# A two-layer hybrid attention kernel: gates moved between the forgetting attention's projections, row-alternating level products, decay rows copied by GpSimd, four equal statistics tiles

## The chip, the cores and the metric

The kernel runs on 1 core of one Trainium2 chip. The metric is the device time of one execution in microseconds (us). Before the change three runs took 1266.27, 1270.57 and 1270.88 us (median 1270.57). The profiled execution took 1268.24 us; its span, from the first to the last instruction, is 1266.4 us.

## The reference, cut to what matters

Everything is fp32. 16 meta tokens and 256 tokens (272 rows, 1024 wide) go through two layers. A layer is a feed-forward block, a token mixer and a second feed-forward block, each between two root-mean-square norms.

```
h = concatenate([meta, x])
for l in range(2):
    h = h + 0.5 * rmsnorm(swiglu(rmsnorm(h), w_ffn1_gu, w_ffn1_down))
    h = h + rmsnorm(token_mixer(rmsnorm(h), ...))
    h = h + 0.5 * rmsnorm(swiglu(rmsnorm(h), w_ffn2_gu, w_ffn2_down))
```

The mixer multiplies the normed rows by one wide matrix `w_in` and splits the product into queries, keys and values of two attentions and into three sets of gates:

```
log_f = log_sigmoid(ff + b_f)                      # 8 heads, forgetting attention ("fox")
s = q k^T / 8 + cum[q] - cum[k]                    # cum = cumsum(log_f)
o_fox = softmax(masked s) v
log_a = log_sigmoid(ga @ w_alpha_up + b_alpha)/16  # 4 heads, gated linear attention ("gla")
o_gla = chunked linear attention with a decay exp(cb[t] - cb[s]) per key channel
o_gla = rmsnorm(o_gla) * silu(gr)
y = sigmoid(g_merge_a) * (o_fox @ w_fox_o) + sigmoid(g_merge_b) * (o_gla @ w_gla_o)
return y @ w_out
```

## The kernel before

All activations lie transposed: 128 of the 1024 features on the partitions, the 272 rows (256 in the last layer's later part) along the free axis. A weight matrix comes by DMA in blocks of 128 x 1024 fp32 (SP's queue, `w`). Each half block of 512 columns is split into a rounded part (`wh`, an ACT cast, line 106) and the rest (`wl`, a DVE subtraction, line 112), and the operand likewise (`xh`, `xl`). A product of 128 features by 128 features is then three matmuls (`mm3`, lines 122 to 124: wh·xh, wh·xl, wl·xh), and a block makes 24 of them into one PSUM bank. Twelve half-block buffers let ACT and DVE run ahead of TensorE.

`inv_rms` makes a norm's factor. The squares of the features, already added up over the eight feature tiles, are summed over partitions by matmuls with a column of ones (line 171), so that the 272 sums land on partitions: two tiles of 128 and one of 16. DVE scales them (`ms`, line 179, once for the full tiles and once for the tile of 16), GpSimd raises them to -1/2 (`rp`, line 180), and matmuls against the identity (line 183) spread them over all partitions again. An fp32 matmul is two passes in the profile, a transpose one. `inv_rms` is called in `prep` (before each block of a layer, amid TensorE's projections) and in `Post.done` (after each block; there nothing else is left to do, and `idle` puts 5 and then 8 matmuls of no use around the broadcast). Of the eleven calls nine have 272 rows, two 256; the four of `Post.done` with 272 rows have two summands each.

The mixer's first four weight blocks give the decay inputs, the gla keys and half of its queries. After them comes a list `proj` of 37 blocks: the other half of the gla queries; for each of four head pairs the fox keys, queries and values; four blocks of gla values; the output gate `gr` (4); and the merge gates `ag` and `bg` (8 each, in turn). Each block's bank is emptied by one or two DVE instructions (lines 427, 436, 438, 450, 490). Two banks `mm` take turns, so a block waits until the block two before it has been emptied.

The attention's own steps are put between these blocks by `at(i, step)`: the step is written out just ahead of block i. `scores(b)` (line 645, the matmuls of two heads, then the softmax on DVE and ACT), `turn_fox`, `turn_scores` and `weigh` (the transposes and products with the values) stand three blocks apart for the four head pairs. `level(i)` makes the gla operand E of one of seven block widths L = 64 ... 1 on DVE and ACT; `products(i)` then multiplies its parts (line 562) and copies them into `att` by a mask. A head's operand has 64 rows: heads 0 and 2 lie on partitions 0 to 63, heads 1 and 3 on 64 to 127, r = 0 or 1 in the code. In layer 0 the levels of width 8 and less and `diagonal` (line 588) also have the 16 meta rows, whose stationary operand is 16 columns wide (lines 565 and 590). A scheduler with its own model of time then orders the instructions of every engine; each engine runs them in that order.

In `decays` the logarithms of the forget gates are made for 8 heads on partitions 32 to 39 and summed along the rows (the scan at line 416, `cf`). They enter the scores as extra rows of the contraction: `qa` has cum in rows 96 to 103 and marks in 64 to 71, `ka` has -cum (line 420) in 64 to 71 and marks in 96 to 103. Two DMAs issued by ACT (lines 421 and 422) spread these rows over 8 heads, so that scores contract over 104 rows, of which 48 are zeros or marks set by GpSimd (lines 344 to 347).

All sigmoids of the gates are put behind the last exponential by `follows`, so that ACT seldom changes its table.

## Time and profile before

| what | value |
|---|---|
| three runs | 1266.27, 1270.57, 1270.88 us |
| profiled execution, its span | 1268.24 us, 1266.4 us |
| TensorE (PE) busy | 1247.4 us, 99% |
| VectorE (DVE) busy | 893.4 us, 71% |
| ScalarE (ACT) busy | 697.5 us, 55% |
| GpSimd (POOL) busy | 34.9 us, 3% |
| TensorE's granted clock | 0.9 of full or more in every fortieth of the span |
| chain that ended last | PE 82%, "issue" 14%, DMA 1%, ACT 1% |

Matmuls are pipelined: one takes about 0.29 us from its start to its end, and the next starts about 0.125 us after it. A busy time of PE counts overlapped ends, so what an instruction costs is read from the distance between starts in the timeline, not from its duration.

### The profile page before, as it was taken

How to read it: one execution, taken by the hardware profiler on the slowest of the kernel's cores; microseconds unless marked ns; L12 is line 12 of the kernel's file. 1: busy time of each engine (PE TensorE's matmuls, PEld its weight loads, DVE VectorE, ACT ScalarE, POOL GpSimd, SP SyncE). 2: the span in 40 equal slices, each digit the busy share in tenths (PEclk: the TensorE clock that was granted, in tenths of full speed). 3: DMA queues.
4: the chain of work that ended last, by engine and by line, in shares of the span. 5: the costliest groups of instructions: out<-in, count | busy, mean ns of one | idle time of the engine just before them, and what ended most of it. 6: DMA issues, size and time to landing. Idle time of an engine off the chain costs nothing.

```text
span 1266.4 us, 25250 instructions
## 1 busy us (share of the span) xinstructions
PE 1247.4 (99%) x9826; PEld 1210.2 (96%) x9826; DVE 893.4 (71%) x1831; ACT 697.5 (55%) x1451; POOL 34.9 (3%) x43
## 2 busy tenths in 40 slices
PE   7999999999999999999999999999999999999997
PEld 7999999988999999999999999999898999999986
DVE  6777655887567787776568777558986687877662
ACT  7555544764555565554446555446755554755551
POOL 2000000000000100000000000001000000000000
PEclk9999999999999999999999999999999999999999
DMA  9655555443245636556536555564434564665650
GB/s 307 203 171 170 166 175 158 153 119 100 88 138 176 178 126 184 172 170 169 177 114 212 172 178 161 168 192 134 138 96 122 161 185 155 200 187 182 181 166 34
DMA packets 58198, 203.87 MB, mean 161 GB/s; under 512 B 6688, under 2 KB 8000, under 8 KB 58048
## 3 DMA queue, kind: packets, MB, share of 16 engines
q1 hardware_dynamic: 57376, 201.19, 51.7%
q8 instruction: 77, 1.26, 0.4%
q10 hardware_dynamic: 576, 0.80, 0.3%
q14 instruction: 41, 0.34, 0.1%
q0 software_dynamic: 128, 0.28, 0.1%
HBM read 200.92 MB, written 1.05 MB: 159 GB/s over the span
## 4 chain that ended last, share of the span: by engine, by line
PE 82%; issue 14%; DMA 1%; ACT 1%; POOL 0%; SPq 0%; ACTq 0%; DVE 0%; DVEq 0%; POOLq 0%
PE mm L122 13%; PE mm L124 12%; PE mm L123 12%; PE pp L122 7%; PE pp L124 7%; PE pp L123 7%; PE s L122 5%; PE s L123 5%; PE s L124 5%; PE pp L562 1%; PE s L161 1%; PE s L645 1%; DMA w<-in_w_gu 1%; PE po L183 1%; DMA ka<-sm 1%
## 5 line engine op out<-in xcount | busy, mean ns | idle before, releaser
L106 ACT CAST wh<-w 128x512 fp32r<-128x512 f32 (+1 forms) x768 | 464.6, 613 | 414.9 <-PE mm L123 183.8
L112 DVE TENSOR_TENSOR wl<-w,wh 128x512 fp32r<-128x512 f32 (+1 forms) x768 | 516.2, 681 | 246.4 <-ACT wh L106 231.0
L122 PE MATMUL mm<-xh,wh 128*128 128x272 f32 (+1 forms) x1072 | 309.4, 291 | 9.6 <-ACT wh L106 8.7
L124 PE MATMUL mm<-xh,wl 128*128 128x272 f32 (+1 forms) x1072 | 308.8, 289 | 0.0
L123 PE MATMUL mm<-xl,wh 128*128 128x272 f32 (+1 forms) x1072 | 307.8, 288 | 0.0
L122 PEld LDWEIGHTS mm<-xh,wh 128*128 128x128 f32 x1072 | 201.7, 189 | 11.7 <-ACT wh L106 8.9
L123 PEld LDWEIGHTS mm<-xl,wh 128*128 128x128 f32 x1072 | 202.9, 189 | 1.2 <-issue 0.9
L124 PEld LDWEIGHTS mm<-xh,wl 128*128 128x128 f32 x1072 | 202.2, 189 | 1.6 <-issue 1.1
L124 PE MATMUL s<-xh,wl 128*128 128x272 f32 (+1 forms) x496 | 142.2, 287 | 0.0
L123 PE MATMUL s<-xl,wh 128*128 128x272 f32 (+1 forms) x496 | 142.0, 287 | 0.0
L122 PE MATMUL s<-xh,wh 128*128 128x272 f32 (+1 forms) x496 | 141.0, 288 | 0.0
L124 PE MATMUL pp<-xh,wl 128*128 128x272 f32 (+1 forms) x480 | 137.2, 289 | 0.0
L123 PE MATMUL pp<-xl,wh 128*128 128x272 f32 (+1 forms) x480 | 137.0, 288 | 0.0
L122 PE MATMUL pp<-xh,wh 128*128 128x272 f32 (+1 forms) x480 | 134.0, 289 | 0.0
L123 PEld LDWEIGHTS s<-xl,wh 128*128 128x128 f32 x496 | 93.4, 188 | 0.1
L124 PEld LDWEIGHTS s<-xh,wl 128*128 128x128 f32 x496 | 93.4, 188 | 0.0
L122 PEld LDWEIGHTS s<-xh,wh 128*128 128x128 f32 x496 | 92.8, 188 | 0.1
L123 PEld LDWEIGHTS pp<-xl,wh 128*128 128x128 f32 x480 | 90.9, 189 | 0.0
L124 PEld LDWEIGHTS pp<-xh,wl 128*128 128x128 f32 x480 | 90.8, 190 | 0.0
L122 PEld LDWEIGHTS pp<-xh,wh 128*128 128x128 f32 x480 | 89.3, 190 | 0.0
L122 PE MATMUL pp<-hh,wh 128*128 128x272 f32 x264 | 76.1, 288 | 0.0
L122 PE MATMUL mm<-hh,wh 128*128 128x272 f32 x264 | 76.1, 288 | 0.0
(291 smaller groups left out, 2123.9 us busy)
## 6 DMA issues: line engine op xcount, KB each, us to landing
w<-in_w_gu SPq DMA_DIRECT2D x175, 512.0 KB, 3.6
w<-in_w_in SPq DMA_DIRECT2D x82, 512.0 KB, 3.6
w<-in_w_dn SPq DMA_DIRECT2D x48, 512.0 KB, 3.5
w<-in_w_end SPq DMA_DIRECT2D x22, 512.0 KB, 4.0
w<-in_w_dn SPq DMA_DIRECT2D x24, 384.0 KB, 3.5
w<-in_w_fg SPq DMA_DIRECT2D x16, 512.0 KB, 3.6
w<-in_w_o SPq DMA_DIRECT2D x16, 512.0 KB, 3.6
h<-in_xT SPq DMA_DIRECT2D x8, 136.0 KB, 4.7
```

Of the source, the lines that this page charges most:

```text
L106: i = nc.scalar.copy(wh[:, :n], w[:, a:b])
L112: nc.vector.tensor_tensor(wl[:, :n], w[:, a:b], wh[:, :n].bitcast(F32), ALU.subtract)
L122: nc.tensor.matmul(o, a, x[0], start=start, stop=False)
L123: nc.tensor.matmul(o, a, x[1], start=False, stop=False)
L124: nc.tensor.matmul(o, b, x[0], start=False, stop=stop)
L161: m = nc.tensor.matmul(o[:, :P], ident, ident, start=True, stop=True)
L183: last = nc.tensor.matmul(bc[:, o : o + m], rp[:m, j : j + 1].broadcast_to([m, P]), ident[:m, :m], start=True, stop=True)
L562: nc.tensor.matmul(pp[r][:, q * 64 : q * 64 + 64].rearrange("p (b l) -> p b l", l=L), x[:, o : o + P], second(x[:, o : o + P], L), start=T ...
L645: nc.tensor.matmul(s[:, c : c + e], qa[:104, hd, q0:e], ka[:104, hd, 0:e], start=True, stop=True)
```

## The change

`inv_rms` cuts 272 rows into four tiles of 68 (256 into two of 128 as before), needs one DVE instruction for all of them, and spreads the result by transposes instead of matmuls. `operands` and `decays` drop one of the two pairs of extra rows: `qa` has -1 marks in rows 64 to 71, `ka` has cum itself there, written by one GpSimd copy; scores contract over 72 rows. The memsets of rows 64 to 95, one marks DMA, the DVE negation and ACT's two DMAs go. In `products` and `diagonal` the loops go over tile, then head pair, then r, so that neighbouring matmuls lie on different halves of the partitions, and the meta rows' products use a stationary operand of 128 columns and come last. `proj` now puts one gate block after each pair of fox queries and keys and one after each block of values, and all `bg` blocks at the end; the fox steps stand five blocks apart, and the levels and the rest are given later places.

```diff
-        tt = [(o, min(P, n - o)) for o in range(0, n, P)]
-        J = len(tt)
+        m = P if n % P == 0 else n // 4
+        tt = range(0, n, m)
         st = bank("po")
         for i, part in enumerate(parts):
-            for j, (o, m) in enumerate(tt):
+            for j, o in enumerate(tt):
                 last = nc.tensor.matmul(st[:m, j : j + 1], part[:, o : o + m], one, start=i == 0 and j == 0,
...
-        for m, a, b in ((P, 0, n // P), (n % P, n // P, J)):
-            if m and b > a:
-                nc.vector.tensor_scalar(ms[:m, a:b], st[:m, a:b], q / D, q * EPS, ALU.mult, ALU.add)
-        nc.gpsimd.tensor_tensor(rp[:, :J], ms[:, :J], nhalf[:, :J], ALU.pow)
+        nc.vector.tensor_scalar(ms[:m, :J], st[:m, :J], q / D, q * EPS, ALU.mult, ALU.add)
+        nc.gpsimd.tensor_tensor(rp[:m, :J], ms[:m, :J], nhalf[:m, :J], ALU.pow)
         bc = bank("po")
-        for j, (o, m) in enumerate(tt):
-            last = nc.tensor.matmul(bc[:, o : o + m], rp[:m, j : j + 1].broadcast_to([m, P]), ident[:m, :m], start=True, stop=True)
+        for j, o in enumerate(tt):
+            last = nc.tensor.transpose(bc[:, o : o + m], rp[:m, j : j + 1].broadcast_to([m, P]), ident[:m, :m])
...
-        nc.gpsimd.memset(qa[64:96], 0.0)
-        nc.gpsimd.memset(ka[64:96], 0.0)
         nc.gpsimd.dma_start(qa[64:72], marks)
-        nc.gpsimd.dma_start(ka[96:104], marks)
...
-                cf = a[32:40, 2, :]
-                nc.vector.tensor_tensor_scan(cf, one[32:40].broadcast_to([8, NT]), b[32:40, 2, :], 0.0, ALU.mult, ALU.add)
+                    if f0 == 2:
+                        cf = a[rows, 2, :]
+                        nc.vector.tensor_tensor_scan(cf, one[rows].broadcast_to([8, NT]), b[rows, 2, :], 0.0, ALU.mult, ALU.add)
+                        nc.gpsimd.tensor_copy(ka[64:72], cf.unsqueeze(1).broadcast_to([8, FH, NT]))
...
-                nf = sm[32:40]
-                nc.vector.tensor_scalar(nf, cf, -1.0, None, ALU.mult)
-                nc.scalar.dma_start(qa[96:104], cf.unsqueeze(1).broadcast_to([8, FH, NT]))
-                nc.scalar.dma_start(ka[64:72], nf.unsqueeze(1).broadcast_to([8, FH, NT]))
...
+            def both_halves(ks):
+                return [(k, hh, r) for k in range(ks) for hh in range(2) for r in range(2)]
...
-                for hd in range(GH):
-                    r, hh = hd % 2, hd // 2
-                    x = head_rows(E, hd)
-                    for k in range(2):
-                        o = TILES[k + 1][0]
...
-                    if meta:
-                        nc.tensor.matmul(pp[r][:META, 256 + hh * 8 : 264 + hh * 8].rearrange("p (b l) -> p b l", l=L),
-                                         x[:, :META], second(x[:, :META], L), start=True, stop=True)
+                for k, hh, r in both_halves(2):
+                    x = E[64 * r : 64 * r + 64, hh]
+                    o = TILES[k + 1][0]
...
+                for _, hh, r in both_halves(meta):
+                    x = E[64 * r : 64 * r + 64, hh]
+                    nc.tensor.matmul(pp[r][:, 256 + hh * 8 : 264 + hh * 8].rearrange("p (b l) -> p b l", l=L),
+                                     x[:, :P], second(x[:, :META], L), start=True, stop=True)
...
-                        nc.tensor.matmul(s[:, c : c + e], qa[:104, hd, q0:e], ka[:104, hd, 0:e], start=True, stop=True)
+                        nc.tensor.matmul(s[:, c : c + e], qa[:72, hd, q0:e], ka[:72, hd, 0:e], start=True, stop=True)
...
+            gates = [(gate, gr, B_GR + i, i) for i in range(4)] + [(gate, ag, B_MA + i, i) for i in range(KC)]
+            gates.reverse()
             proj = [(gq1,)]
             for i in range(4):
-                proj += [(heads, ka, B_FK + i, i, None), (heads, qa, B_FQ + i, i, FD**-0.5), (values, B_FV + i, i)]
-            proj += [(values, B_GV + i, i) for i in range(4)]
-            proj += [(gate, gr, B_GR + i, i) for i in range(4)]
-            for i in range(KC):
-                proj += [(gate, ag, B_MA + i, i), (gate_b, i)]
+                proj += [(heads, ka, B_FK + i, i, None), (heads, qa, B_FQ + i, i, FD**-0.5), gates.pop(), (values, B_FV + i, i), gates.pop()]
+            for i in range(4):
+                proj += [(values, B_GV + i, i), gates.pop()]
+            proj += [(gate_b, i) for i in range(KC)]
...
-                at(5 + 3 * b, turn_fox, b)
-                at(5 + 3 * b, scores, b)
-                at(6 + 3 * b, turn_scores, b)
-                at(7 + 3 * b, weigh, b)
-            for i in range(len(LEVELS)):
-                at(6 + 2 * i, level, i)
-                at(7 + 2 * i, products, i)
-            at(20, diagonal)
+                at(5 + 5 * b, scores, b)
+                at(7 + 5 * b, turn_fox, b)
+                at(7 + 5 * b, turn_scores, b)
+                at(9 + 5 * b, weigh, b)
+            for i, j in enumerate((5, 7, 10, 12, 15, 17, 20)):
+                at(j, level, i)
+                at(j + 1, products, i)
+            at(23, between_decays)
+            at(23, diagonal)
...
-                at(23 + 2 * i, gla_values, k)
-                at(25 + 2 * i, gla_gate, k)
+                at(30 + 2 * i, gla_values, k)
+                at(32 + 2 * i, gla_gate, k)
```

On TensorE, the level of width 8 in layer 0. Before, with `pp_3776` and `pp_3777` the banks of r = 0 and r = 1, `E` the level's operand and `L667` the transposes of the fox scores:

```order
L562 MATMUL pp_3776<-E_3725 128x64 x2
L565 MATMUL pp_3776<-E_3725 16x8
L562 MATMUL pp_3777<-E_3725 128x64 x2
L565 MATMUL pp_3777<-E_3725 16x8
L562 MATMUL pp_3776<-E_3725 128x64
L667 MATMUL s_3711<-con_70,p_3637 128x128
L562 MATMUL pp_3776<-E_3725 128x64
L667 MATMUL s_3711<-con_70,p_3637 128x128 x2
L667 MATMUL s_3718<-con_70,p_3637 128x128
L565 MATMUL pp_3776<-E_3725 16x8
```

The same level now, from its sixth matmul to the projection that follows it (`pp_3720` and `pp_3721` are r = 0 and 1, L562 the meta rows):

```order
L558 MATMUL pp_3721<-E_3677 128x64
L558 MATMUL pp_3720<-E_3677 128x64
L558 MATMUL pp_3721<-E_3677 128x64
L562 MATMUL pp_3720<-E_3677 128x8
L562 MATMUL pp_3721<-E_3677 128x8
L562 MATMUL pp_3720<-E_3677 128x8
L562 MATMUL pp_3721<-E_3677 128x8
L120 MATMUL mm_3738<-xh_2755,wh_3645 128x272
```

The banks take turns, the meta rows' products are 128 wide and at the end, and the fox transposes stand elsewhere.

On DVE, from the forget gates' logarithms to the operands of the first two levels, layer 0, before (`G` is the gla decays' running sum, `ka_155<-mm_3205` empties the bank of the second block of fox keys' predecessor in turn):

```order
L414 TENSOR_TENSOR lsb_3071<-lsb_3071,lsa_3070 8x272
L112 TENSOR_TENSOR wl_3424<-w_3417,wh_3423 128x512
L416 SCALAR_TENSOR_TENSOR lsa_3070<-ones_71,lsb_3071 8x272
L414 TENSOR_TENSOR lsb_3071<-lsb_3071,lsa_3070 128x544
L420 TENSOR_SCALAR sm_2990<-lsa_3070 8x272
L112 TENSOR_TENSOR wl_3496<-w_3493,wh_3495 128x512
L436 TENSOR_TENSOR ka_155<-mm_3205,rs_2832 64x272 x2
L418 SCALAR_TENSOR_TENSOR G_2993<-ones_71,lsb_3071 128x272 x2
L112 TENSOR_TENSOR wl_3500<-w_3493,wh_3499 128x512
L525 TENSOR_TENSOR E_3327<-G_2993 128x2x2x64
L526 TENSOR_TENSOR E_3327<-G_2993 128x2x2x64
```

The same stretch now, from the forget gates' scan (L412) on (`vt` empties a block of fox values, `gr_3009<-mm_3274` the second output gate's block):

```order
L412 SCALAR_TENSOR_TENSOR lsa_3072<-ones_71,lsb_3073 8x272
L409 TENSOR_TENSOR lsb_3073<-lsb_3073,lsa_3072 128x544
L110 TENSOR_TENSOR wl_3483<-w_3480,wh_3482 128x512
L443 TENSOR_TENSOR vt_3232<-mm_3207,rs_2834 128x272
L415 SCALAR_TENSOR_TENSOR G_2995<-ones_71,lsb_3073 128x272 x2
L110 TENSOR_TENSOR wl_3487<-w_3480,wh_3486 128x512
L110 TENSOR_TENSOR wl_3528<-w_3525,wh_3527 128x512
L518 TENSOR_TENSOR E_3268<-G_2995 128x2x2x64
L519 TENSOR_TENSOR E_3268<-G_2995 128x2x2x64
L518 TENSOR_TENSOR E_3386<-G_2995 128x2x4x32
L519 TENSOR_TENSOR E_3386<-G_2995 128x2x4x32
L483 TENSOR_TENSOR gr_3009<-mm_3274,rs_2834 128x272
```

The negation is gone, and a gate's bank is emptied only after both levels' subtractions.

On TensorE, the sums after the mixer of layer 0 before (`sq` the squares, `s<-con` the idle matmuls):

```order
L171 MATMUL po_5636<-ones_71,sq_5595 128x1 x2
L171 MATMUL po_5636<-ones_71,sq_5595 16x1
L171 MATMUL po_5636<-ones_71,sq_5634 128x1 x2
L171 MATMUL po_5636<-ones_71,sq_5634 16x1
L161 MATMUL s_5643<-con_70 128x128 x5
L183 MATMUL po_5653<-con_70,rp_5649 128x128 x2
L183 MATMUL po_5653<-con_70,rp_5649 128x16
L161 MATMUL s_5657<-con_70 128x128 x8
```

And now:

```order
L169 MATMUL po_5636<-ones_71,sq_5595 68x1 x4
L169 MATMUL po_5636<-ones_71,sq_5634 68x1 x4
L159 MATMUL s_5645<-con_70 128x128 x5
L180 MATMUL po_5655<-con_70,rp_5652 128x68 x4
L159 MATMUL s_5660<-con_70 128x128 x8
```

Four tiles of one size stand where two of 128 and one of 16 stood; the rows L180 are transposes.

## Rows read from the trace of the kernel before

**Rows 1.** Page, part 1: busy us, share of the span, instructions of each engine.
```profile
PE 1247.4 (99%) x9826; PEld 1210.2 (96%) x9826; DVE 893.4 (71%) x1831; ACT 697.5 (55%) x1451; POOL 34.9 (3%) x43
```

**Rows 2.** Waits of PE: who waited for whom, us in total, times, longest.
```profile
PE s L645 <- DMA ka<-sm: 2.1, 2, 1.1
PE mm L122 <- DVE ka L436: 0.9, 2, 0.6
```

**Rows 3.** Timeline of PE, layer 0, level of width 4 (start us, us, instruction).
```profile
302.06 0.66 PE L562 MATMUL pp<-E 64*128 64x64 f32 x4
302.65 0.21 PE L565 MATMUL pp<-E 64*16 64x8 f32 x2
...
304.94 0.39 PE L122 MATMUL mm<-xh,wh 128*128 128x272 f32 x1
```

**Rows 4.** Timeline of PE, layer 1, level of width 1, without meta rows.
```profile
959.12 1.16 PE L562 MATMUL pp<-E 64*128 64x64 f32 x16
960.21 0.39 PE L122 MATMUL mm<-xh,wh 128*128 128x256 f32 x1
```

**Rows 5.** Timeline of PE, the diagonal products, layer 0 and then layer 1.
```profile
331.40 0.71 PE L588 MATMUL pp<-gq,gk 64*128 64x128 f32 x4
332.04 0.21 PE L590 MATMUL s<-gq,gk 64*16 64x16 f32 x2
...
334.52 0.39 PE L122 MATMUL mm<-xh,wh 128*128 128x272 f32 x1
...
963.24 1.26 PE L588 MATMUL pp<-gq,gk 64*128 64x128 f32 x16
```

**Rows 6.** Timeline of PE, the broadcast of the first norm's factor.
```profile
24.72 0.93 PE L183 MATMUL po<-con,rp 128*128 128x128 f32 x6
25.58 0.39 PE L122 MATMUL pp<-xh,wh 128*128 128x272 f32 x1
```

**Rows 7.** Timeline of PE, four transposes of 128 rows (line 762).
```profile
369.79 0.60 PE L762 MATMUL s<-con,on 128*128 128x128 f32 x4
370.15 0.37 PE L122 MATMUL mm<-xh,wh 128*128 128x272 f32 x1
```

**Rows 8.** Timeline of PE, the first norm's sums over partitions.
```profile
20.42 0.63 PE L171 MATMUL po<-ones,sq 128*128 128x1 f32 x6
20.98 0.39 PE L123 MATMUL mm<-xl,wh 128*128 128x272 f32 x1
```

**Rows 9.** Timeline of PE, layer 0, from behind the decay products to the first scores.
```profile
244.00 0.40 PE L123 MATMUL mm<-xl,wh 128*128 128x272 f32 x1
...
252.10 0.29 PE L123 MATMUL mm<-xl,wh 128*128 128x272 f32 x1
...
253.35 0.29 PE L124 MATMUL mm<-xh,wl 128*128 128x272 f32 x1
254.77 1.64 PE L645 MATMUL s<-ka,qa 104*128 104x144 f32 x8 [1.13 <-DMA ka<-sm]
```

**Rows 10.** Timeline of DVE, layer 0, the stretch shown above in its order.
```profile
247.06 0.43 DVE L414 TENSOR_TENSOR lsb<-lsb,lsa 8x272 f32<-8x272 f32 x1 [1.32 <-ACT lsa L412]
...
249.93 0.29 DVE L420 TENSOR_SCALAR sm<-lsa 8x272 f32<-8x272 f32 x1
...
250.87 0.88 DVE L436 TENSOR_TENSOR ka<-mm,rs 64x272 f32<-64x272 f32 x2
...
254.63 0.42 DVE L526 TENSOR_TENSOR E<-G 128x256 f32<-128x256 f32 x1
```

**Rows 11.** Timeline of POOL: two powers and one memset.
```profile
214.89 0.85 POOL L180 TENSOR_TENSOR rp<-ms,nhalf 128x3 f32<-128x3 f32 x1
232.70 2.38 POOL L180 TENSOR_TENSOR rp<-ms,nhalf 128x3 f32<-128x3 f32 x1 [16.95 <-DVE ms L179]
...
421.29 1.94 POOL L344 MEMSET qa<- 32x2176 f32 x1
```

**Rows 12.** Timeline of DVE beside the second of these powers.
```profile
232.49 1.87 DVE L112 TENSOR_TENSOR wl<-w,wh 128x512 fp32r<-128x512 f32 x3
```

More of the change, by code (lines that the diff above doesn't have):

```diff
@@ L71, in hybrid_kernel @@
     one = ones[:, 0:1]
-    ms = cp.tile([P, 4], F32, name="ms")
-    nc.gpsimd.memset(ms, 1.0)
     nhalf = cp.tile([P, 4], F32, name="nhalf")
@@ L555, in products @@
                 mask = con[:, C_LVL + i * P : C_LVL + (i + 1) * P].bitcast(I32)
-                for hd in range(GH):
-                    r, hh = hd % 2, hd // 2
-                    x = head_rows(E, hd)
-                    for k in range(2):
-                        o = TILES[k + 1][0]
-                        q = 2 * k + hh
-                        nc.tensor.matmul(pp[r][:, q * 64 : q * 64 + 64].rearrange("p (b l) -> p b l", l=L), x[:, o : o + P],
-                                         second(x[:, o : o + P], L), start=True, stop=True)
-                    if meta:
-                        nc.tensor.matmul(pp[r][:META, 256 + hh * 8 : 264 + hh * 8].rearrange("p (b l) -> p b l", l=L),
-                                         x[:, :META], second(x[:, :META], L), start=True, stop=True)
+                for k, hh, r in both_halves(2):
+                    x = E[64 * r : 64 * r + 64, hh]
+                    o = TILES[k + 1][0]
+                    q = 2 * k + hh
+                    nc.tensor.matmul(pp[r][:, q * 64 : q * 64 + 64].rearrange("p (b l) -> p b l", l=L), x[:, o : o + P],
+                                     second(x[:, o : o + P], L), start=True, stop=True)
+                for _, hh, r in both_halves(meta):
+                    x = E[64 * r : 64 * r + 64, hh]
+                    nc.tensor.matmul(pp[r][:, 256 + hh * 8 : 264 + hh * 8].rearrange("p (b l) -> p b l", l=L),
+                                     x[:, :P], second(x[:, :META], L), start=True, stop=True)
                 for r in range(2):
@@ L581, in diagonal @@
                 mask = con[:, C_LVL + i * P : C_LVL + (i + 1) * P].bitcast(I32)
-                for hd in range(GH):
-                    r, hh = hd % 2, hd // 2
-                    xk, xq = head_rows(gk, hd), head_rows(gq, hd)
-                    for k in range(2):
-                        o = TILES[k + 1][0]
-                        q = 2 * k + hh
-                        nc.tensor.matmul(pp[r][:, q * P : (q + 1) * P], xk[:, o : o + P], xq[:, o : o + P], start=True, stop=True)
-                    if not c0:
-                        nc.tensor.matmul(p0[r][:META, hh * META : (hh + 1) * META], xk[:, :META], xq[:, :META], start=True, stop=True)
+                for k, hh, r in both_halves(2):
+                    xk, xq = gk[64 * r : 64 * r + 64, hh], gq[64 * r : 64 * r + 64, hh]
+                    o = TILES[k + 1][0]
+                    q = 2 * k + hh
+                    nc.tensor.matmul(pp[r][:, q * P : (q + 1) * P], xk[:, o : o + P], xq[:, o : o + P], start=True, stop=True)
+                for _, hh, r in both_halves(not c0):
+                    xk, xq = gk[64 * r : 64 * r + 64, hh], gq[64 * r : 64 * r + 64, hh]
+                    nc.tensor.matmul(p0[r][:, hh * META : (hh + 1) * META], xk[:, :P], xq[:, :META], start=True, stop=True)
                 for r in range(2):
@@ L693, in meta_scores @@
                 for hd in range(FH):
-                    nc.tensor.matmul(s[:, hd, :], qa[:104, hd, :META], ka[:104, hd, :META], start=True, stop=True)
+                    nc.tensor.matmul(s[:, hd, :], qa[:72, hd, :META], ka[:72, hd, :META], start=True, stop=True)
                 one_mask = cmask[:META, 144:160].unsqueeze(1).broadcast_to([META, FH, META])
@@ L784, in mixer @@
             for b in range(4):
[L785 to L792 removed]
+                at(5 + 5 * b, scores, b)
[7 more added lines that the diff above has]
+            at(23, diagonal)
+            at(26, between)
             if not c0:
[L794 to L797 removed]
+                at(25, meta_scores)
+                at(28, meta_weigh)
             for i in range(4):
[L799 removed]
+                at(23 + 2 * i, turn_gla, i)
             ks = (1, 2) if c0 else (0, 1, 2)
             for i, k in enumerate(ks):
[L802 to L803 removed]
+                at(30 + 2 * i, gla_values, k)
+                at(32 + 2 * i, gla_gate, k)
             for i, (f, *a) in enumerate(proj):
@@ L925, in pack @@
         "consts": constants(),
-        "marks": np.ascontiguousarray(np.broadcast_to(np.eye(FH, dtype=np.float32)[:, :, None], (FH, FH, NT))),
+        "marks": np.ascontiguousarray(np.broadcast_to(-np.eye(FH, dtype=np.float32)[:, :, None], (FH, FH, NT))),
     }
```

10 lines of the change are left out of this document (3 added, 7 removed).

## The prediction

> **What bounds the kernel now.** I read the page's busy times first, then the waits of TensorE, then TensorE's timeline where the change touches it, and last DVE and GpSimd around the one wait that the change removes. The reader is to see in [rows 1] that TensorE is busy 99% of the span, while DVE has 29% and ACT 45% free, and in [rows 2] that only 3.0 us of TensorE's waits in the whole run lie in the mixers: 2.1 for the DMA that brings the decay rows and 0.9 for a bank that DVE empties late. So time is won by taking TensorE's own time away; what DVE, ACT and GpSimd save is worth something only where TensorE waits for them. Since busy times overlap, I price everything from one start in the timeline to the start of what follows.
>
> **Term 1: the level products of layer 0.** In layer 0 the level of width 4 runs from 302.06 to 304.94, 2.88 us: per head four passes of 64x128 and two of 64x16, one after the other [rows 3]. In layer 1, without the meta rows, sixteen passes of the same size take from 959.12 to 960.21, 1.09 us, 0.068 us a pass [rows 4]: there the heads of the two partition halves run beside each other. The difference of 1.79 us is far more than eight small passes are worth; it is the switch between stationary operands 128 and 16 columns wide that keeps the halves apart. The diagonal says the same: 331.40 to 334.52, 3.12 us in layer 0, 1.26 in layer 1 [rows 5]. After the change all passes have 128 stationary columns, the halves take turns, and the meta rows add eight passes. I price them like the others, 8 x 0.068 = 0.54. A level then takes 1.09 + 0.54 = 1.63 instead of 2.88, and four levels have meta rows (8, 4, 2, 1): 4 x 1.25 = 5.0 us. The diagonal takes 1.26 + 0.54 = 1.80 instead of 3.12: 1.3 us. Together 6.3. Bounds: 9.0 if the meta passes cost nothing (4 x 1.79 + 1.86), 0 if the halves still do not overlap. I take 6.3, since [rows 4, 5] show the same operation. Layer 1 has no meta rows there, overlaps already, and gains nothing. Its cover is not needed: TensorE itself is what is saved.
>
> **Term 2: spreading the norm's factor.** Six passes before, 24.72 to 25.58, 0.86 us [rows 6]; four transposes after. Four transposes of 128 rows take 369.79 to 370.15, 0.36 us [rows 7]; one of 68 rows should cost no more. That is 0.50 us in each of nine calls, 4.5 us. The two calls with 256 rows go from four passes to two transposes; by half I take 0.25 each, 0.5. In `prep` TensorE is amid projections, so its time is saved directly; in `Post.done` the broadcast stands in the chain from the sum to the first operand of the next block, and the eight idle matmuls behind it only move with it. Together 5.0. Bounds: 0 if a transpose of a broadcast operand costs as much as two passes, 6.6 if one of 68 rows costs half of one of 128 (0.18 less in nine calls).
>
> **Term 3: the sums over partitions.** Six passes, four of 128 columns and two of 16, take 20.42 to 20.98, 0.56 us [rows 8]. Eight passes of 68 columns take their place. If a pass goes by its columns, and the four wide ones had taken all of the 0.56 (0.14 each), one of 68 takes 0.075 and eight take 0.60: no change. No row shows a pass of 68. If it costs a full 0.14, thirteen summands lose 13 x 0.56 = 7 us; if the passes come as close as those of the levels (0.068) [rows 4] or closer, at 0.04, they gain 13 x 0.24 = 3. I take 0, the value by columns. One of DVE's two `ms` instructions goes too; in `Post.done` the five idle matmuls cover it, and in `prep` the projections do, so it counts as nothing.
>
> **Term 4: the decay rows.** The negation (0.29) [rows 10], ACT's two DMA issues and the DMA itself go, and with them the 2.1 us of [rows 2]. What is late next is DVE. Behind the decay products TensorE restarts at 244.00 with a pace of 0.125 us a matmul (ten from 252.10 to 253.35) [rows 9]. By the new order it makes 78 projections until the second block of fox queries, which would be at 244.00 + 9.75 = 253.75; that block needs the bank of the second output gate. DVE empties it only behind both levels' subtractions. Before, DVE went from 247.06 to 254.63 + 0.42 = 255.05 to the end of these [rows 10]. Now the negation (0.29) and the fox keys (0.88) are not in between, but one block of values (0.44, half of the 0.88 for two) and one more split (0.62) [rows 12] are: 254.94, and 255.4 with the gate's own 0.44. So TensorE waits 1.6 us there, where it waited 1.1 + 0.3 in layer 0. In layer 1 the gate is emptied one subtraction (0.4) earlier, 1.2 us, against 0.9 + 0.6. Together 2.8 instead of 3.0: I take a gain of 0.2. Queued behind the waiting matmul on TensorE are that block, the first level's products and the first scores, so nothing else of the mixer can fill the gap. The GpSimd copy of 8 x 2176 elements is not in the trace: at least the 1.94 us of a memset of as many elements, at most that stretched as a power was beside DVE (0.85 to 2.38) [rows 11], 5.4 us. It starts where the negation did, 249.93, and the scores come a block after the gate, at about 255.4 + 3.0 = 258.4. So 8.5 us cover it at either end; without that cover its excess would stand in front of the scores in both layers.
>
> What else moves is covered. The memsets and the marks DMA of GpSimd fall where it idles (3% busy). By the order the exponentials and sigmoids change ACT's table twice more in layer 1, with 45% of ACT free. The last step of the gated linear attention now stands one block before the projections end, but 48 matmuls (6.0 us) lie between its transposes and the first product that reads them, against three operations of 512 columns on DVE, ACT and DVE (about 0.62 each, an estimate from [rows 12]). Scores over 72 instead of 104 rows have the same columns and passes: nothing, either way.
>
> **The sum.** 6.3 + 5.0 + 0 + 0.2 = 11.5 us less. Against the profiled execution's own 1268.24 that is 1256.7, so I forecast 1257. The profiled execution lies 2.3 below the median of the three runs (1270.57) and inside their spread.
>
> **The rivals.**
> (a) The waits go altogether: the scheduler's order holds and DVE keeps up, as its 29% of idle time would allow. For it: after the first third of the mixer no wait of TensorE appears in [rows 2]. Against: the count of term 4. It gives 2.8 us more, 1254.
> (b) The GpSimd copy holds DVE up. It reads SBUF while DVE splits weights, and every us of DVE is on TensorE's path there (term 4). Over its length in both layers that costs 2 x 1.94 to 2 x 5.4, 1261 to 1268. Against: beside the stretched power DVE's three splits took 1.87, 0.62 each [rows 11, 12], so there GpSimd gave way and not DVE. The Trainium skill (SBUF — State Buffer, Who interferes with whom) has the rule that a DVE instruction with two SBUF inputs and a GpSimd instruction that reads SBUF cannot run together: whichever starts first keeps the shared ports for its whole length. By that rule a long copy that once gets in stops DVE until its end, and this rival would be the case; the trace shows the contention, but only with DVE as the winner.
> (c) The halves don't overlap in the new order, so that it does not do what it says: term 1 is gone, 1263. Against: [rows 4, 5], which show the overlap without the narrow operand. For: there four passes of one half came together, now two.
> (d) Slower: gates are emptied late all through the mixers. The change puts twelve gate blocks per layer between the fox steps, and with two banks each one that DVE empties late stops TensorE, as the second output gate does in term 4 (1.6 us). If the other 22 wait like it, they cost 35 us, 1292. It decides from 0.8 us a gate on, where 22 x 0.8 = 17.6 outweighs the 11.5 and the 6.4 that can be told. Against: in the order later gates stand next to the splits of their own time, not behind a chain of decays.
>
> **How the numbers follow.** The forecast has 0.60, (a) 0.15, (b) 0.15, (c) 0.06, (d) 0.04. The forecast's own range is 1252 to 1262, from term 3 (-3 to a few us, a full-width price being far from its row) and the meta passes. The range of 8 in 10 takes in (a) and most of (b) and (c): 1250 to 1265. What a measurement of this kernel can tell is about 0.5%, 6.4 us: faster is below 1264.2, slower above 1276.9. The forecast and (a) are faster but for 0.02, (b) in 0.09 of its 0.15 and (c) in 0.02: 0.84. (d) is slower, 0.04. The rest, 0.12, is the same.
>
> **What would show it.** In the profile after, a level with meta rows from its first pass to the next projection should take about 1.6 us, the diagonal 1.8; if a level still takes 2.9, term 1 is wrong. The broadcast should take about 0.36 us to the next projection, the sums about 0.6. There should be no wait for a DMA at the scores, but one of 1 to 2 us at a projection, for DVE emptying an output gate, once per layer. A GpSimd copy over 3 us with a DVE split several times its 0.62 beside it would be (b). Waits for gates at many blocks would be (d). If terms 1 and 2 come out and the time does not fall by some 11 us, the loss must stand among TensorE's waits.

## The result, and the profile after

The changed kernel takes 1256.01 us (median; 1252.37 to 1256.23) against 1268.93 for the kernel before (four runs, one more than above): a ratio of 0.9892 [0.987, 0.9913], faster by 12.9 us. The forecast was 1257. The profiled execution took 1256.23 (span 1254.2) against 1268.24, 12.0 less. Executions of one kernel differ by some 6 us with the clock that TensorE was granted: of 23 of the kernel before, those with a mean granted clock of 0.998 or 0.999 took 1266.6 to 1267.3 us, those with 0.993 took 1271.5 to 1273.2.

Part 1 of the page after, which answers to [rows 1], and then TensorE's waits, which answer to [rows 2]:

```profile
PE 1230.3 (98%) x9830; PEld 1197.8 (96%) x9830; DVE 894.3 (71%) x1820; ACT 698.7 (56%) x1453; POOL 32.8 (3%) x38
```

```profile
PE mm L120 <- ACT wh L104: 8.5, 2, 7.7
PE po L180 <- POOL rp L177: 2.2, 5, 1.3
PE mm L120 <- DVE gr L483: 2.1, 1, 2.1
PE mm L120 <- DVE vt L443: 2.1, 2, 1.7
PE s L664 <- ACT pk L653: 1.2, 1, 1.2
PE s L663 <- DVE p L651: 0.5, 1, 0.5
```

TensorE is busy 17 us less, but its waits in the mixers grew: the DMA wait is gone, and DVE (`gr`, `vt`) and ACT (`pk`) are waited for instead. Of the first line 0.87 us lie in the mixer of layer 0, the rest at the start. The waits for `rp`, the norm's power, are new too; 1.26 of their 2.2 us stand at the first norm. The timeline of TensorE after shows the edits themselves: the sums and then the broadcast of the first norm (as [rows 8, 6]), the level of width 4 of layer 0 (as [rows 3]), and the diagonal of layer 0 (as [rows 5]).

```profile
17.96 0.60 PE L169 MATMUL po<-ones,sq 128*68 128x1 f32 x8
18.42 0.37 PE L120 MATMUL pp<-xh,wh 128*128 128x272 f32 x1
...
23.93 0.45 PE L180 MATMUL po<-con,rp 68*128 68x68 f32 x4 [1.26 <-POOL rp L177]
24.18 0.37 PE L122 MATMUL s<-xh,wl 128*128 128x272 f32 x1
...
296.71 1.11 PE L558 MATMUL pp<-E 64*128 64x64 f32 x16
297.65 0.57 PE L562 MATMUL pp<-E 64*128 64x8 f32 x8
298.14 0.39 PE L120 MATMUL mm<-xh,wh 128*128 128x272 f32 x1
...
328.01 1.16 PE L583 MATMUL pp<-gq,gk 64*128 64x128 f32 x16
329.01 0.52 PE L586 MATMUL s<-gq,gk 64*128 64x16 f32 x8
329.46 0.50 PE L463 MATMUL s<-con,vt 128*16 128x128 f32 x3
```

From start to start a level takes 1.43 us (2.88 before), the diagonal 1.45 (3.12), the sums 0.46 (0.56), the broadcast 0.25 (0.86). All four are a little better than forecast.

What was not forecast stands on DVE beside GpSimd's copy. First GpSimd, then DVE, layer 0 and layer 1:

```profile
246.18 2.45 POOL L413 COPY ka<-lsa 8x2176 f32<-8x2176 f32 x1 [14.83 <-ACT wh L104]
...
879.22 1.99 POOL L413 COPY ka<-lsa 8x2176 f32<-8x2176 f32 x1 [15.93 <-DVE lsa L412]
```

```profile
246.04 0.72 DVE L409 TENSOR_TENSOR lsb<-lsb,lsa 128x544 f32<-128x544 f32 x1
246.69 2.48 DVE L110 TENSOR_TENSOR wl<-w,wh 128x512 fp32r<-128x512 f32 x1
...
879.09 0.44 DVE L443 TENSOR_TENSOR vt<-mm,rs 128x272 f32<-128x272 f32 x1
879.45 2.96 DVE L415 TENSOR_TENSOR_SCAN G<-ones,lsb 128x272 f32<-128x272 f32 x2
```

One split takes 2.48 us instead of some 0.68, two scans 2.96 instead of 1.34 (before). Each ends as if it had begun when the copy ended: 246.18 + 2.45 = 248.63, and 248.63 + 0.68 is close to the split's end at 249.17; 879.22 + 1.99 = 881.21, and 881.21 + 1.34 is close to 882.41. `vt` reads PSUM and one SBUF operand, overlaps the copy and keeps its 0.44.

In layer 0 the copy itself had started 0.14 us behind a subtraction with two SBUF inputs (`lsb`), took 0.46 longer than in layer 1, and still got in ahead of the split. The power of the first norm did not get in between seven splits. On GpSimd, then DVE:

```profile
18.91 4.97 POOL L177 TENSOR_TENSOR rp<-ms,nhalf 68x4 f32<-68x4 f32 x1 [16.34 <-ACT wh L104]
```

```profile
18.67 4.29 DVE L110 TENSOR_TENSOR wl<-w,wh 128x512 fp32r<-128x512 f32 x7
```

TensorE waits behind the copies, and in layer 1 its granted clock is halved after the wait (timeline, then the view of stretches, where the next to last but one figure is the clock):

```profile
249.67 0.36 PE L120 MATMUL mm<-xh,wh 128*128 128x272 f32 x1 [1.73 <-DVE vt L443]
...
885.08 0.36 PE L120 MATMUL mm<-xh,wh 128*128 128x256 f32 x1 [2.14 <-DVE gr L483]
```

```profile
885.74:889.12 3.38, 3.38 (x18) 3.38 (x17) 3.34 (x9) 0.85 (x2) 0.00 (x0) 0.50 0.64 185
```

3.38 us at 0.50 (1.2 GHz) do the work of 1.69: 1.7 us more behind the wait of 2.14. The wait of 1.73 in layer 0 has no such stretch behind it.

The last loss is on ACT in layer 1, at the last scores:

```profile
947.01 1.09 ACT L350 ACTIVATE ex<-ex 128x1056 f32<-128x1056 f32 x1
948.11 1.28 ACT L479 ACT_TABLE_LOAD   x1
949.41 0.72 ACT L479 ACTIVATE sg<-gr 128x256 f32<-128x256 f32 x2
...
951.07 1.28 ACT L350 ACT_TABLE_LOAD   x1
952.37 0.41 ACT L350 ACTIVATE p<-p,mn 128x144 f32<-128x144 f32 x1
...
953.91 1.28 ACT L479 ACT_TABLE_LOAD   x1
```

Sigmoids need only follow the program's last exponential, `ex`. The schedule ran `ex` before the last scores, so sigmoids came in between, at 949.41, and the scores' exponentials came at 952.37, two table loads later. TensorE's waits for `p` (0.53) and `pk` (1.22) are these.

To compare kernels part by part I cut every trace at the start of each norm's sums on TensorE (us; "rest" ends where TensorE's last matmul starts):

```
kernel         first sums  ffn1 layer 0  mixer 0  mixer 1   rest
before              20.42        192.68   211.10   191.99  642.94
after               17.96        193.04   204.38   193.42  638.31
only_levels         18.29        192.76   205.08   191.60  642.89
turns_narrow        18.92        192.78   204.25   191.60  642.94
width_alone         18.37        192.78   208.15   191.86  642.95
only_norm           18.27        191.86   209.79   197.80  638.31
only_order          20.08        192.69   213.96   191.07  642.86
only_rows           18.16        193.97   215.70   195.88  642.76
row_dma_pool        17.31        191.58   201.16   189.81  638.34
all_exps            18.29        193.04   204.38   191.22  638.39
both                17.80        193.03   201.15   187.66  638.36
both_narrow         17.49        193.03   200.16   187.62  638.46
both_no_norm        17.27        195.47   202.11   187.62  642.83
twice               17.77        191.58   206.18   196.71  638.39
```

Before to after: -2.46, +0.36, -6.72, +1.43, -4.63, together the 12.0. "Rest" repeats to 0.2 us among kernels with the same norm, so a difference there is the norm's. The start does not repeat (17.3 to 20.4), so the 2.5 us ahead of the first sums are not put down to any part. A stretch at half clock from 16.62 to 20.03, which cost 1.7 us, is in them: of all these traces only those of before and only_order have one there.

### The profile page after: what moved, and what is told of

Same layout as the page of the kernel before. It is cut to its first block, busy times and chain, and to the rows that moved or that the text cites. A ratio compares the mean times of both kernels' runs of the same rounds, so it can differ in the third digit from the quotient of the medians.

```text
span 1254.2 us, 25185 instructions
## 1 busy us (share of the span) xinstructions
PE 1230.3 (98%) x9830; PEld 1197.8 (96%) x9830; DVE 894.3 (71%) x1820; ACT 698.7 (56%) x1453; POOL 32.8 (3%) x38
## 3 DMA queue, kind: packets, MB, share of 16 engines
q8 instruction: 77, 1.26, 0.4%
## 4 chain that ended last, share of the span: by engine, by line
PE 80%; issue 15%; ACT 1%; DVE 1%; POOL 1%; DMA 1%; SPq 0%; DVEq 0%; POOLq 0%
PE mm L120 13%; PE mm L121 12%; PE mm L122 12%; PE pp L121 7%; PE pp L120 7%; PE pp L122 7%; PE s L121 5%; PE s L122 5%; PE s L120 5%; PE s L641 1%; PE s L159 1%; PE pp L558 1%; POOL rp L177 1%; DMA w<-in_w_gu 1%; PE po L738 1%
```

## The experiments

All were timed in five rounds against the kernel before on the same chip. Not all ran on one chip, so it is their ratios that compare.

**Levels: turns and width.** Three kernels made from the one before. only_levels has the whole edit, turns_narrow keeps the 16-column operand, width_alone the old order:

```diff
-                for hd in range(GH):
+                for k, hh, r in both_halves(2):
...
+                for _, hh, r in both_halves(meta):
...
-                                         x[:, :META], second(x[:, :META], L), start=True, stop=True)
+                                     x[:, :P], second(x[:, :META], L), start=True, stop=True)
```

The first three lines are the turns, the last two the width.

> The kernel before with one part of the change alone: the level products and the diagonal, where the two partition halves take turns and the passes for the meta rows have a stationary operand of 128 columns. By my theory (term 1: the narrow operand kept the halves apart) TensorE's time for a level with meta rows falls from 2.9 to about 1.6 us and for the diagonal of layer 0 from 3.1 to 1.8, in all 6.3 us less than before: a ratio of 0.995. The trace of the whole change showed 8.3 us less on these lines (19.36 to 12.84 and 4.31 to 2.54, from start to start), so 0.9935 if all of that comes from this part. By the rival, that most of it came from the new places in the order, it is under 2 us: 0.9985 or more.

> As only_levels (the halves take turns, meta passes behind the others), but the meta passes keep their stationary operand of 16 columns. If the switch of width between 128 and 16 columns is what costs, there is now one switch in a level instead of four or more, and the wide passes overlap: a level takes about 1.1 us for the wide passes and up to 0.9 for the eight narrow ones (0.11 each), 2.0 in all, so some 4 to 5 us of the 6.3 are gained (ratio 0.9965). If turns are the whole cause, it gains as much as only_levels, 6.3 to 8.3 us. If the width is the whole cause and a narrow operand anywhere in the group keeps the halves apart, it gains nothing (1.000).

> The kernel before with the meta operand made 128 columns wide and nothing else: heads in the old order, two wide passes and the meta pass of a head together. With turns_narrow this separates the two halves of the levels' edit. By my term 1 (the switch between 128 and 16 columns keeps the halves apart) a level with meta rows now takes 1.6 us instead of 2.9: as much as only_levels, 8 us less, of which 6 in the mixer of layer 0, ratio 0.9935. By the rival that turns_narrow speaks for (what matters is that the meta passes come behind the others and the halves alternate), it gains under 2 us, 0.9985 or more.

Measured: only_levels 0.993 [0.9912, 0.9948], turns_narrow 0.9921 [0.9903, 0.9939], width_alone 0.9952 [0.9935, 0.9969]. The intervals hold part of the uncertain start; mixer 0 tells them apart: -6.0, -6.9 and -3.0. One level in turns_narrow:

```profile
299.50 1.11 PE L565 MATMUL pp<-E 64*128 64x64 f32 x16
300.54 0.26 PE L569 MATMUL pp<-E 64*16 64x8 f32 x8
300.74 0.40 PE L122 MATMUL mm<-xh,wh 128*128 128x272 f32 x1
```

It takes 1.24 us with the narrow operand, 1.43 with the wide one (after). So the narrow operand does no harm where its passes stand behind the wide ones: a switch of width by itself is not the cause. In the old order, with a switch at every head, the width does matter: in width_alone the level of width 4 runs from 301.16 to 302.87, 1.71 us instead of 2.88. Either edit ends most of the serial passes of the old level; the turns do it better. Over all levels and the diagonals, from start to start, width_alone saves 4.5 of 26.3 us, only_levels 6.7, turns_narrow 8.2. In mixer 0 width_alone gained less than this, since a stretch at half clock stands behind the level of width 8 and the meta scores (290.63 to 293.57, 1.5 us lost).

**The norm alone,** in the kernel before:

```diff
-        tt = [(o, min(P, n - o)) for o in range(0, n, P)]
+        m = P if n % P == 0 else n // 4
+        tt = range(0, n, m)
...
-            last = nc.tensor.matmul(bc[:, o : o + m], rp[:m, j : j + 1].broadcast_to([m, P]), ident[:m, :m], start=True, stop=True)
+            last = nc.tensor.transpose(bc[:, o : o + m], rp[:m, j : j + 1].broadcast_to([m, P]), ident[:m, :m])
```

> The kernel before with the norm's part alone: equal tiles (four of 68 columns, or two of 128), transposes for the broadcast, one instruction for the mean. Terms 2 and 3: 5.0 us less, 0 for the sums; ratio 0.996. The trace of the whole change has 6.4 us less on the broadcast line and 1.1 less on the sums, 7.5 in all, so 0.994 if nothing of it is given back. The rival says that the broadcast behind a block stands in a chain with GpSimd's power, and that the power now starts no earlier or runs longer beside the splits (4.97 us for the first one in the trace after, 1.2 before): then up to 3 us come back, 0.9965.

Measured 0.999 [0.9976, 1.0003], less than either expected. The profiled execution took 1264.93 us at a granted clock of 0.998; the twelve go from there to 1273.2 at 0.990. The table says where it went: rest -4.6, ffn1 -0.8, mixer 0 -1.3, but mixer 1 +5.8. DVE, ACT's queue and TensorE there:

```profile
884.71 1.34 DVE L415 TENSOR_TENSOR_SCAN G<-ones,lsb 128x272 f32<-128x272 f32 x2
885.97 0.67 DVE L110 TENSOR_TENSOR wl<-w,wh 128x512 fp32r<-128x512 f32 x1
886.67 0.29 DVE L417 TENSOR_SCALAR sm<-lsa 8x272 f32<-8x272 f32 x1
```

```profile
886.99 0.69 ACTq L419 DMA_DIRECT2D ka<-sm  x1
```

```profile
891.45 2.56 PE L642 MATMUL s<-ka,qa 104*128 104x144 f32 x8 [3.36 <-DMA ka<-sm]
```

The schedule put the negation behind both scans (before, it stood ahead of them), so the DMA left late, and TensorE waited 3.36 us (0.94 before) and went on at half clock for 3.4, which cost 1.7. These are 4.1 of the 5.8; the rest I have not followed. The norm's gain is real; it was given back in a place that the norm does not touch.

**The order alone,** with all its places, of which these are two:

```diff
-                at(5 + 3 * b, scores, b)
+                at(5 + 5 * b, scores, b)
...
-                at(6 + 2 * i, level, i)
+                at(j, level, i)
```

> The kernel before with the new order of the blocks alone: gates between the fox projections, fox steps five apart, levels at their new places; decay rows still by DMA. My term 4 had the new order's gate waits cost 2.8 us and save the 3.0 of the DMA and the fox keys: no change, 1.000. The trace of the whole change has 5.75 us of waits behind the decays and 1.9 for the last scores of layer 1, where sigmoids came before the last exponentials and ACT changed its table twice more. If the GpSimd copy held DVE for 3.4 of the 5.75 (a wl split of 2.48 instead of 0.68 us and two G scans of 2.96 instead of 1.34 beside it), the order alone has some 2.4 + 1.9 = 4.3 us of waits against 3.0, +1.3: ratio 1.001. If instead the gates' places cost all 5.75, it is +4.6: 1.0036.

Measured 0.998 [0.9967, 0.9994]; mixer 1 -0.9, mixer 0 +2.9, though TensorE waits less in mixer 0 than before (0.6 us for the DMA, before 1.1 and 0.3); in mixer 1 it waits 0.2 for the DMA, 0.5 for `vt` and 1.7 at the last scores. The profiled execution took 1269.71 us at a granted clock of 0.994; the twelve go from 1265.11 at 0.997 to 1271.33 at 0.992. The view of stretches shows what the profiled one lost in mixer 0:

```profile
286.56:289.73 3.17, 3.17 (x16) 3.17 (x15) 1.77 (x7) 1.28 (x2) 0.00 (x0) 0.50 0.35 129
...
303.52:306.69 3.17, 3.17 (x15) 3.17 (x15) 1.39 (x4) 1.18 (x2) 0.00 (x0) 0.50 0.33 131
...
330.68:334.07 3.39, 3.39 (x18) 3.39 (x16) 1.78 (x7) 0.76 (x2) 0.00 (x0) 0.50 0.51 155
```

9.7 us at 0.50 cost 4.9. Each begins within 1.2 us of the end of a level, the first behind one whose narrow and wide passes ran one after the other from 283.34 to 286.22. In the traces of the kernels with the turns none stands behind a level; the trace of before has the same slow levels and none either. But executions of before differ from 0.993 to 0.999 in their granted clock, so one trace does not tell what a kernel does on average. What decides it is open.

**The decay rows alone:**

```diff
+                        nc.gpsimd.tensor_copy(ka[64:72], cf.unsqueeze(1).broadcast_to([8, FH, NT]))
...
-                nc.scalar.dma_start(qa[96:104], cf.unsqueeze(1).broadcast_to([8, FH, NT]))
-                nc.scalar.dma_start(ka[64:72], nf.unsqueeze(1).broadcast_to([8, FH, NT]))
```

> The kernel before with the decay rows' part alone: GpSimd copies the rows into the keys, the marks are negative, scores over 72 rows. Theory A, that the copy holds DVE (a split beside it took 2.48 us instead of 0.68 and two scans 2.96 instead of 1.34 in the trace of the whole change): the DMA wait of 2.1 us goes, the waits for the fox keys grow from 0.9 by 1.8 and 1.6 less twice the negation's 0.29, so waits of some 3.7 us against 3.0: +0.7, ratio 1.0005, and up to 1.7 more where a wait over 2 us is followed by a stretch at half the clock, 1.002. Theory B, that the copy is harmless: 2.1 us less, 0.998.

Measured 1.0046 [1.0028, 1.0064]: slower by 5.6 us, theory A by its direction and too small by its size. The split beside the copy took 2.49 and 2.48 us. Its delay is paid at two places in each layer, at the fox keys and again at the queries:

```profile
PE mm L122 <- DVE ka L432: 3.6, 2, 2.0
PE mm L122 <- DVE qa L434: 3.1, 2, 1.5
```

6.7 us of waits against 3.0, and two stretches at half clock in mixer 0 (3.18 and 2.04 us, 2.6 lost). Another 1.3 us were lost in the first feed-forward block, where TensorE waited 1.28 us for a power of 4.78 us; the copy has no part in that.

**The copy taken away, and doubled,** in the changed kernel. row_dma_pool:

```diff
-                        nc.gpsimd.tensor_copy(ka[64:72], cf.unsqueeze(1).broadcast_to([8, FH, NT]))
+                        nc.gpsimd.dma_start(ka[64:72], cf.unsqueeze(1).broadcast_to([8, FH, NT]))
```

twice:

```diff
                         nc.gpsimd.tensor_copy(ka[64:72], cf.unsqueeze(1).broadcast_to([8, FH, NT]))
+                        nc.gpsimd.tensor_copy(ka[64:72], cf.unsqueeze(1).broadcast_to([8, FH, NT]))
```

> The whole change, with one edit: instead of GpSimd's copy one DMA, issued by GpSimd, brings the decay row to the keys (72 rows, no negation, as after). Theory A (the copy holds DVE): the split and the scans beside it take 0.68 and 1.34 us again, the waits behind the decays (1.73 and 0.87 in layer 0, 0.40 and 2.14 in layer 1) fall by up to 1.8 and 1.6, and the stretch at half clock behind the 2.14 (1.7 us) goes: 3.4 to 5 us less than the whole change, some 1251 to 1253, 0.987 against before. Theory B (the waits are those of the gates' places): the same as the whole change, 0.9895. The DMA has some 11 us until the first scores and lands in about 4.

> The whole change with GpSimd's copy of the decay row made twice, one behind the other, to the same place. Theory A (a copy that has started holds DVE until its end): a second hold of 2.0 to 2.4 us in each layer, if the second copy gets in ahead of DVE, so 4 to 5 us more waits and up to 1.7 in each layer at half the clock: 1260 to 1264, 0.993 to 0.996 against before. If DVE gets in between the two, the second copy waits and is late for nothing: DVE is held a second time only in part, +0 to 4. Theory B (the copy is harmless): 0.9895 as the whole change.

Measured: row_dma_pool 0.9844 [0.9827, 0.986], 1248.74 us, 7.3 less than the whole change (6.1 by the ratios); twice 0.9921 [0.9903, 0.9939], 1259.66, 3.7 more. DVE in row_dma_pool, at the two places shown above:

```profile
244.57 0.68 DVE L110 TENSOR_TENSOR wl<-w,wh 128x512 fp32r<-128x512 f32 x1
...
874.13 1.33 DVE L415 TENSOR_TENSOR_SCAN G<-ones,lsb 128x272 f32<-128x272 f32 x2
```

With two copies, on GpSimd and DVE in layer 1:

```profile
881.42 2.31 POOL L414 COPY ka<-lsa 8x2176 f32<-8x2176 f32 x1
```

```profile
879.60 4.71 DVE L416 TENSOR_TENSOR_SCAN G<-ones,lsb 128x272 f32<-128x272 f32 x2
```

Without the copy the split and the scans have their old durations; with two the scans take 4.71. Theory A holds, at 6.8 us (mixer 0 -3.2, mixer 1 -3.6), more than the 3.4 to 5 expected. Another 1.5 us of row_dma_pool's gain are in the first feed-forward block, where the first power took 1.35 us instead of 4.97; the copy has no part in that. The second copy held DVE for another 1.44 us in layer 0 and 1.75 in layer 1; the mixers took 5.1 us more, and the whole, with 3.7, lies a little under theory A's 4 to 8. The gate wait that I had forecast does not exist without the copy. What is left behind the decays in row_dma_pool:

```profile
PE s L641 <- DMA ka<-lsa: 0.4, 1, 0.4
PE mm L120 <- DVE vt L443: 0.4, 1, 0.4
```

**Sigmoids behind the last nine exponentials,** in the changed kernel (all_exps) and in row_dma_pool (both):

```diff
 for a in late:
-    follows(a, exps[-1], ONE_CHANGE)
+    for e in exps[-9:]:
+        follows(a, e, ONE_CHANGE)
```

> The whole change, with one edit: every sigmoid of a mixer follows the last nine exponentials of the program instead of the very last one. In the trace of the whole change ACT takes sigmoids of layer 1 from 948.11 on, before the last two exponentials of the scores (952.37), with two table loads more, and TensorE waits 0.53 and 1.22 us behind them. If the table loads are the cause, one load is left there, both waits go and 1.5 to 1.9 us are gained: 1254, 0.988 against before. If the last scores are late for another reason (DVE's share of them), nothing changes: 0.9895. If the later sigmoids hold up the gates' buffers, it is slower by a us or two.

> The whole change with both edits, the DMA for the decay row and the sigmoids behind all exponentials. If both causes hold they lie in different places of the mixer and add up: 3.4 to 5 and 1.5 to 1.9 us less than the whole change, some 1249 to 1251, ratio 0.985 against before. If only one holds, 1251 to 1254.

Measured: all_exps 0.9874 [0.9855, 0.9892], both 0.9832 [0.9817, 0.9847], 1247.22 us. The first interval overlaps that of the whole change, so the trace decides: mixer 0 unchanged, mixer 1 -2.2, with and without the copy. The two edits add up, as expected: both has 9.0 us less in the mixers than the whole change (4.9 to 6.9 expected). ACT in all_exps:

```profile
947.32 1.09 ACT L350 ACTIVATE ex<-ex 128x1056 f32<-128x1056 f32 x1
948.31 0.40 ACT L350 ACTIVATE p<-p,mn 128x144 f32<-128x144 f32 x1
...
949.33 1.28 ACT L479 ACT_TABLE_LOAD   x1
```

**The best version, and the norm without its accident.** both_no_norm is both without the diff of only_norm; both_narrow is both with the narrow operand:

```diff
-                                     x[:, :P], second(x[:, :META], L), start=True, stop=True)
+                                     x[:, :META], second(x[:, :META], L), start=True, stop=True)
```

> The kernel called both (the whole change, the decay row by DMA, sigmoids behind all exponentials) with the meta operand at 16 columns again, in the new order. In turns_narrow the eight meta passes of a level took 0.26 us against some 0.5 to 0.6 of the wide ones, and layer 0's mixer was 0.8 us shorter than in only_levels. So 0.8 to 1 us less than both: some 1246.3, 0.9825 against before. If the narrow passes break the overlap in the new places, 1 to 6 us more.

> The kernel called both with the norm of the kernel before (uneven tiles, matmuls for the broadcast). Stage by stage the norm's part took 0.4 to 0.9 us off each stretch outside the mixers, some 6.5 us in all, but alone it was worth 0.8 us, since in its layer 1 the scheduler put the negation behind both scans and the DMA of the decay rows became late (wait 3.4 us and a stretch at half the clock). If that is why, then without that DMA path the norm is worth its 6.5: this kernel 1253.7, 0.988 against before. If the norm gives its gain back everywhere, it is as fast as both, 0.983.

Measured: both_narrow 0.9808 [0.9785, 0.9831], 1245.2 us, the lowest of all, though its interval overlaps that of both; in the traces mixer 0 is 1.0 shorter, as expected. both_no_norm 0.9875 [0.9854, 0.9896], 1254.29: the norm is worth 0.0043, 5.5 us, here (some 3 more or less by the two intervals), against 0.8 alone.

## Why the prediction was right, and where it was not

**The total came out by errors that cancel.** The 12.9 us are 1.4 more than my sum, and that they are so close is luck. Of the 12.0 us between the two traces 2.5 lie ahead of the first sums and are no term of mine. The other 9.6 are two losses of 9.0 together (the copy 6.8, the table changes 2.2) that my sum did not have, and so gains of about 18.6 where I had 11.5.

**Term 1, right in size.** Forecast -6.3; only_levels has -6.0 in mixer 0 and -0.4 in mixer 1. Its reason was half right: the passes did run apart, but it needs the narrow passes between the heads; the narrow operand behind them does no harm.

**Terms 2 and 3, mis-sized.** Forecast -5.0 and 0. both against both_no_norm: rest -4.5, mixers -0.9; with only_norm's -0.8 in ffn1, -6.2. A broadcast saves 0.61 and not 0.50, since 68 rows cost less than 128, and the sums gain 0.10, since passes of 68 columns take 0.058 each. Both lie inside my bounds. What I had not seen is that TensorE now waits for the power: 2.2 us in five calls. The 1.26 of the first call, behind a power of 4.97 us, account for ffn1 being 0.36 longer in after and not 0.8 shorter as in only_norm.

**Term 4, the failed step.** I took -0.2: waits of 1.6 and 1.2 us for an output gate, and the copy covered. Measured are waits of 1.73 + 0.87 and 0.40 + 2.14, and 1.7 us at half clock. The cause is rival (b), to which I gave 0.15. The copy costs 6.8 us in the mixers, inside its own 3.9 to 10.8, though not as I had priced it: the copies were short (2.45 and 1.99 us, where my upper end and my sign of (b) had over 3), and 1.7 us are the halved clock. The wait for `gr` that I had named as a sign is there, but it comes from the copy. I had asked when the copy's result is needed, and for that 8.5 us were cover enough; I set aside whom it stops while it runs. My argument against it was a power on a few elements that gave way to three splits [rows 11, 12]. After, a power beside seven splits took 4.97 us, while the copies won over the split and the scans. In each case the one that had got in kept the other out; why the power could not get in between two of the splits, and the copies could behind `lsb` and, by its times in twice, between the two scans, no run shows. The rows bear out the rule of the Trainium skill (SBUF — State Buffer, Who interferes with whom): a DVE instruction with two SBUF inputs contends with a GpSimd instruction that reads SBUF, one with at most one SBUF input, outside its two-port modes, does not. Split, scan and `vt` agree with it. That the second waits for the whole length of the first, as the prediction had it, the section says of the two-port modes; the rows above show it for the split and the scans. The DMA in the copy's place, which GpSimd only issues, left the split at 0.68.

**Not priced at all.** The table changes, set to nothing because 45% of ACT is free: 2.2 us, since they stood between the last scores and TensorE. The halved clock behind a long wait. On the other side, what the order gives: from before to both the mixers fall by 14.3 us, of which the levels are 6.4, the norm 0.9 and the waits of [rows 2] less what is left about 2; the other 5 are left for the new order. Some 3 of them are on the turns of the scores and the products between tiles (start to start 7.58 to 5.84 and 3.57 to 2.42 us, before to after; only_order has 6.14 and 2.42), and 2.3 on the levels and diagonals themselves (19.7 in only_levels, 17.4 in both). That this is from better neighbours on TensorE is only argued. Nor did I price the granted clock of whole executions: its median is 0.995 to 0.996 in the four kernels with the old levels (before, only_norm, only_order, only_rows) and 0.997 to 0.999 in the others, but for twice with its longer waits (0.996). One thousandth is about 1.3 us of this span, an estimate. That the old levels are the cause is only argued.

**Why the parts don't add up.** Alone they gave -8.3, -0.8, -1.5 and +5.6, together -5.0, while the whole gave -12.9. The norm's loss stands on the old DMA path, as both_no_norm bears out, and the stretches at half clock in the traces of only_order and only_rows lie in mixer 0, where the old levels still stand. So it seems that each part removes places where another lost its gain; of the clock this is only argued, since it differs between executions of one kernel.

**The other rivals.** (a) is what row_dma_pool shows: with the copy gone, so are the waits behind the decays but for 0.85 us. (c) is excluded by the levels. (d) did not happen: no other gate is waited for. (Its limit of 0.8 us a gate was slightly low: 17.6 does not outweigh 11.5 + 6.4 = 17.9.)

## What to carry to other kernels

Price a helper engine's instruction also by whom it stops while it runs: two GpSimd copies of 2.0 and 2.5 us, for whose result nothing waited, cost 7 us through DVE, and a DMA for the same bytes a wait of 0.45. Measure a part of a change by stage and not by the total alone, since a schedule made anew can give its gain back elsewhere. An order between two classes of work has to name every member of the first class, not the one that the program writes last.

## What the hardware showed that was not expected

- Waits of 2.14 (after), 2.31 and 3.90 (twice) and 3.36 us (only_norm) on TensorE were followed by stretches at a granted clock of 0.50, of which the first lasted 3.38 us; behind waits of 1.73 (after) and 1.96 (only_rows, layer 1) there is none. The length alone does not decide it: behind the wait of 1.26 at the first norm's broadcast both_no_norm has such a stretch, and after has none. Such stretches also stood behind levels, without a wait, in only_order, only_rows and width_alone.
- Eight half-height passes with a 16-column operand took 0.20 us when they stood together behind wide ones, and the same passes between wide ones kept the two halves apart.
- A change of ACT's table costs its load alone here: `ex` ends at 948.10, the load runs from 948.11 for 1.28 us, the next activation starts at 949.41. The Trainium skill (ScalarE: Activation LUTs, What ACT_TABLE_LOAD costs) has the same load of 1283 ns, and a drain of about 1380 ns beside it that these rows do not show.
